# A decoder layer on one core: raw weight blocks of the summed operands on GpSimd's DMA queue, another split of the buffers, and sums three chunks ahead

## The chip, the cores and the metric

The kernel runs on one core of one Trainium2 chip. The time is the device time of one execution in microseconds (us); of several runs the median counts. The engines are called PE (TensorE, the matrix multiplications; PEld is its loading of weights), DVE (VectorE), ACT (ScalarE), POOL (GpSimd) and SP (SyncE, which here only issues DMAs). POOL issues DMAs too, through a queue of its own.

## The reference

One decoder layer for 256 tokens of width 2048, all in float32. `h = rmsnorm(x)` is multiplied by one wide matrix `w_in`, and the product is cut into seven parts:

```python
x_r, g_r, q, k, v, gate_r, gate_a = jnp.split(h @ w_in, ...)
y_r = (gelu(g_r) * rg_lru(conv(x_r), ...)) @ w_rnn_out
y_a = stick_breaking_attention(norm(q), norm(k), v) @ w_attn_out
x = x + (sigmoid(gate_r) * y_r + sigmoid(gate_a) * y_a) @ w_o
g, u = jnp.split(rmsnorm(x) @ w_ffn_gu, 2)
x = x + (silu(g) * u) @ w_ffn_down
x = x + sigmoid(rmsnorm(x) @ w_ple_gate) * (p @ w_ple_proj)
```

The weights are by far most of the bytes: about 400 MB cross from HBM in one execution.

## The kernel before

**Precision.** Each float32 weight `w` is cut on the chip into `whi = round(w)` (ACT, line 347) and `wlo = w - whi` (DVE, line 348), both in a shorter format that PE multiplies fast. Activations are cut in the same way. A product is then three matmuls: hi with hi, hi with lo, lo with hi (lines 622 to 624).

**Stages.** The order of the weights is fixed by `plan()`: first a gate (`gtr`), then the recurrent branch (loops over 11 pairs of column tiles), then the stages of `tail()`: `ro` (out of the recurrent branch), `v`, eight blocks for q and k with the attention between them, four blocks for the attention's gate (`gta`), `ao` (attention out), `wo`, and the FFN: groups `gu` 0 to 3, `dn0`, `gu` 4 to 7, `dn1`, `gu` 8 to 10, `dn2`; at last `pg`. A stage of the tail has one or two groups of columns, and a group is a list of slots (`SEVEN3`, `SEVEN4`, `LONG`, `TWELVE`). A slot is a plain chunk of 1024 weight columns (512 KB), or one with a name ("11", "T1", "22", ("S", 2, p), ...).

**Sums.** The named slots are a Strassen-like scheme: seven products of half-size blocks take the place of eight, and for that sums of raw weight blocks are needed. `Stream.dma_to` (line 243) loads a raw block of such a slot into a buffer of the large kind ("Q"), with SP's queue like all other weights (line 263). `Stream.summed` (line 268) adds blocks on DVE (line 273). Further terms are added by `joins` (line 306): a DMA from POOL's queue that adds onto what lies in the buffer (line 310).

**Look-ahead.** For each chunk that PE takes, `need` (line 360) issues loads up to 8 chunks ahead, splits up to 4 chunks ahead and sums up to `SUMS_AHEAD` = 2 chunks beyond those splits. `EARLY` moves the raw blocks of some groups four chunks forward in the order of the loads. Plain weights go through 4 buffers `w32` and 5 pairs `whi`/`wlo`.

**Buffers.** All other tiles come from two kinds: 29 of 1024 columns ("Q", 4 KB a partition) and 21 of 512 columns ("H"). The kind is picked by the tag of `tl` (line 413): "C" and "T" are H, all others Q. The eight tiles of the attention's gate are H.

**Order.** The engines' lists are made by a scheduler when the program is built; within a list an engine goes strictly in order. `issue_after` pins a piece behind another instruction of the same engine; `behind_splits` (line 850) pins it behind the latest split.

**V.** The tiles of `v` are scaled by the tokens' norms and split again (lines 940 to 946): one ACT and one DVE instruction for each of 8 tiles, written after each of the two groups.

Of the kernel before, what the change touches and what calls it, by code (L numbers as in the profile page):

```python
# [31 lines left out]
NG = 11  # L32
# [7 lines left out]
TWO = (0, 1)  # L40
FOUR = ("gu", "v")
LAST_GROUP = ("pg", 1)
SUMS_AHEAD = 2
TURNED_FROM = {"ao": 5, "wo": 5, "pg": 5}
EARLY = {(n, g): 4 for n in ("ro", "v", "wo", "pg") for g in range(2)}
NEG = -1e30


# [8 lines left out]
def is_sum(x):  # L57

    return isinstance(x, str) or isinstance(x, tuple) and x[0] == "S"
# [14 lines left out]
C_XR, C_GR, C_Q, C_K, C_V, C_GTR, C_GTA = 0, 22, 44, 60, 76, 92, 108  # L74
# [155 lines left out]
CHUNK_OF = {PLAN[c[0]][0][1:]: j for j, c in enumerate(CHUNKS) if PLAN[c[0]][0][0] == "tok"}  # L230


class Stream:


    def __init__(self, nc, w, p32, phl, quad, ahead_dma, ahead_split):
        self.nc, self.w, self.quad = nc, w, quad
        self.p32, self.phl = p32, phl
        self.ad, self.asp = ahead_dma, ahead_split
        self.n_dma = self.n_sum = self.n_split = self.pos = 0  # L240
        self.raw, self.sums, self.of, self.parts, self.after = {}, {}, {}, {}, {}

    def dma_to(self, n):
        n = DMA_UPTO[min(n, len(CHUNKS))]
        while self.n_dma < n:
            j = DMA_ORDER[self.n_dma]
            i, a, b = CHUNKS[j]
            c = P * (b - a)
            mode = PLAN[i][0][3] if PLAN[i][0][0] == "tok" else 0
            if is_sum(mode):  # L250
                if c:
                    t = self.quad()
                    self.raw[PLAN[i][0][1:]] = t
            else:
                if j in HALVES:
                    t = self.raw[j - 1][1][:, 512:]
                    self.raw[j] = t, None
                else:
                    t = self.p32.tile([P, 1024], F32, tag="w32", name=f"w32_{j}")
                    self.raw[j] = t, t  # L260
            if c:
                src = self.w[OFFS[j]:OFFS[j] + P * c].rearrange("(p c) -> p c", p=P)
                self.nc.sync.dma_start(t[:, :c], src)
            self.n_dma += 1
            if j in self.after:
                self.after.pop(j)()

    def summed(self, key):


        *at, mode = key
        r = self.raw
        add = lambda o, a, b: self.nc.vector.tensor_tensor(o, a, b, ALU.add)  # L273
        g = lambda m: (*at, m)
        if isinstance(mode, tuple):
            _, i, p = mode
            if i == 2:
                y = r[g(("Y", p))] = self.quad()
                a, b = r.pop(g(("S", 1, p))), r[key]
                add(y[:, :512], a[:, :512], b[:, 512:])  # L280
                add(y[:, 512:], y[:, :512], b[:, :512])
                self.joins(b, 512, g(("S", 2, p)), 0)
                return y, 1024
            if i == 3:
                return r.pop(g(("S", 2, p))), 1024
# [12 lines left out]
        if mode == "T3":  # L298
            return r.pop(g("12")), 1024
        if mode == "T4":  # L300
            return r.pop(g("R")), 1024
        t = r[g("R")]
        add(t, t, r[g("22")])
        return t, 1024

# [94 lines left out]
def tile_hybrid_block(ctx: ExitStack, tc: tile.TileContext, xT: bass.AP, x: bass.AP, pT: bass.AP,  # L400
                      prm: bass.AP, w: bass.AP, out: bass.AP):
    nc = tc.nc
# [4 lines left out]
    stat = ctx.enter_context(tc.tile_pool(name="stat", bufs=2))  # L407
    pps = ctx.enter_context(tc.tile_pool(name="pps", bufs=8, space=bass.MemoryType.PSUM))

    NT = {"Q": (29, 1024), "H": (21, 512)}  # L410
    cnt = [0]

    def tl(tag, dt=F32):
        cnt[0] += 1
        tag = "H" if tag in "CT" else "Q"
        n, c = NT[tag]
        return act.tile([P, c], dt, tag=tag, name=f"{tag}_{cnt[0]}", bufs=n)
# [5 lines left out]
    def f32(ap):  # L423
        return ap.bitcast(F32)
# [4 lines left out]
    def stt(o, a, s, b, op0, op1):  # L429
        nc.vector.scalar_tensor_tensor(o, a, s, b, op0, op1)  # L430

    def actv(o, i, f, **kw):
        nc.scalar.activation(o, i, f, **kw)  # L433

    S_ = Stream(nc, w, p32, phl, lambda: tl("X"), 4, 4)

    def load_x(t, i):
        nc.sync.dma_start(t, xT[:, 2 * i:2 * i + 2, :].rearrange("p k s -> p (k s)"))
# [27 lines left out]
    warm = psum()  # L466
    for i in range(8):
        nc.tensor.matmul(warm, blank[:, :P], blank, start=True, stop=True)
    ones = cst.tile([P, P], F32, tag="ones", name="ones")
    with tc.issue_after(m.ins):  # L470
        nc.vector.memset(ones, 1.0)
    eps_t = cst.tile([P, 1], F32, tag="eps", name="eps_t")
# [3 lines left out]
    zero_t = cst.tile([P, 1], F32, tag="zero", name="zero_t")  # L476
    nc.vector.memset(zero_t, 0.0)

    ones_r = cst.tile([P, P], F32R, tag="onesr", name="ones_r")
    nc.vector.tensor_copy(ones_r, ones)  # L480
    tmp = tl("T")
    later_r = cst.tile([P, P], F32R, tag="laterr", name="later_r")
    nc.gpsimd.affine_select(tmp[:, :P], ones, [[-1, P]], ALU.is_gt, 0.0, base=0, channel_multiplier=1)
# [180 lines left out]
    xg = []  # L664
# [172 lines left out]
    def rs_x(t):  # L837
        return rstd_tok[:, t:t + 1]

    def sigmoids(pss, tag):  # L840
        ts = [tl(tag) for _ in range(2)]
        for t, ps in enumerate(pss):
            actv(ts[t], ps, AF.Sigmoid, scale=rs_x(t))
        return ts

    def gate(c0, b, tag, step=None):
        return sigmoids(block(c0, b, step), tag)

    @contextmanager
    def behind_splits():  # L850
        with tc.issue_after(S_.hi_ins.ins), tc.issue_after(S_.lo_ins.ins):
# [54 lines left out]
    def whole(at, pairs, sums, also=()):  # L906

        (q2, q4, q3, q8), t = group(at, pairs, sums, None, also)
        c11, c21, c12, c22 = t["11"], t["T2"], t["T1"], t["T3"]
        tt(c11, q2, c11, ALU.add)  # L910
        tt(c21, q4, c22, ALU.add)
        tt(c12, q3, c12, ALU.add)
        tt(c22, q8, c22, ALU.subtract)
        return c11, c21, c12, c22
# [21 lines left out]
            tt(o, c, o, ALU.mult)  # L936
    mix_r = gtr

    vs = []
    for g in range(2):  # L940
        for i, c in enumerate(whole(("v", g), xg, xsum)):
            r = rs_x(i % 2)
            v = tl("B", F32R)
            actv(v[:, :512], c, AF.Identity, scale=r)
            stt(v[:, 512:], c, r, f32(v[:, :512]), ALU.mult, ALU.subtract)
            vs.append(v)


    qs, ks, zst, ost = {}, {}, {}, []
# [126 lines left out]
        slot[0] += 1  # L1076

    for b in range(4):
        head_norms(C_Q, b, step)
        head_norms(C_K, b, step)  # L1080
    gta = [gate(C_GTA, b, "T", step) for b in range(4)]
    assert not at

    mix, msum = [], {}
# [238 lines left out]
```

## Time and profile before

| what | us |
|---|---|
| runs | 1864.57, 1865.04, 1867.91 |
| median of the runs | 1865.04 |
| the profiled execution, as timed | 1866.62 |
| span of the profiled execution | 1864.7 |
| PE busy in it | 1851.0 |
| DVE busy | 1486.3 |
| ACT busy | 1244.0 |
| POOL busy | 117.1 |

The profile is of one execution. Its span runs from the first to the last instruction; the time around it is 1.92 us. PE's busy time counts a matmul from start to modelled end, and these overlap; so a late matmul costs the distance of the starts, which is a little more than the idle time that the profile names.

### The profile page before, as it was taken

Reading aid. Unit: us, or ns where it says so; the run is one execution under the profiler, and the core shown is the slowest. Engines: PE = TensorE matmul, PEld = TensorE weight load, DVE = VectorE, ACT = ScalarE, POOL = GpSimd, SP = SyncE. Lnnn points to the kernel's source line nnn. Section 1 sums busy time; section 2 is a strip of 40 time slices with the busy share of each in tenths; the row PEclk is TensorE's granted clock in tenths of the full one; section 3 lists DMA queues with packets and bytes.
Section 4 is the critical chain, followed back from the end, with each engine's and each line's share of the span. In section 5 each row is a group of like instructions: output and inputs, shape, how many; then the busy total and the mean of one; then the engine's idle time right before and its main releaser. Section 6 shows DMA issues by size and latency. Waiting matters only on the chain.

```text
span 1864.7 us, 24660 instructions
## 1 busy us (share of the span) xinstructions
PE 1851.0 (99%) x8882; PEld 1550.7 (83%) x8882; DVE 1486.3 (80%) x1874; ACT 1244.0 (67%) x1672; POOL 117.1 (6%) x142
## 2 busy tenths in 40 slices
PE   9999999999999999999999999999999999999998
PEld 7899889888878888888888878888788888888887
DVE  7688887677887576667798988897888988889986
ACT  6587888775565566667666776665656665666774
POOL 0000000000010000000000011100111001011000
PEclk9999999999999999999999999999999999999999
DMA  8546555677866544556777878787877669678674
GB/s 285 183 175 185 192 188 198 244 234 212 308 152 201 189 167 148 168 166 238 211 237 241 280 231 254 223 270 251 268 238 234 207 221 334 191 223 255 197 236 147
DMA packets 121370, 409.64 MB, mean 220 GB/s; under 512 B 13600, under 2 KB 14240, under 8 KB 121248
## 3 DMA queue, kind: packets, MB, share of 16 engines
q1 hardware_dynamic: 101808, 359.82, 53.6%
q0 software_dynamic: 19296, 48.24, 15.0%
q8 instruction: 69, 1.13, 0.2%
q14 instruction: 53, 0.43, 0.1%
q10 hardware_dynamic: 144, 0.01, 0.0%
HBM read 405.92 MB, written 2.10 MB: 219 GB/s over the span
## 4 chain that ended last, share of the span: by engine, by line
PE 90%; DMA 4%; DVE 4%; issue 1%; ACT 1%; SPq 0%; DVEq 0%; ACTq 0%
PE ps L623 24%; PE ps L624 24%; PE ps L622 24%; PE ps L552 9%; PE ps L556 5%; DMA Q<-in_w_dram 2%; DMA w<-in_w_dram 2%; DVE wlo L348 2%; PE ps L536 1%; PE ps L535 1%; PE ps L534 1%; DVE H L427 1%; ACT whi L347 0%; PE ps L1198 0%; PE ps L979 0%
## 5 line engine op out<-in xcount | busy, mean ns | idle before, releaser
L623 PE MATMUL ps<-wlo,Q 128*128 128x512 f32 x2184 | 852.1, 391 | 4.8 <-DVE wlo L348 4.7
L624 PE MATMUL ps<-whi,Q 128*128 128x512 f32 x2184 | 849.2, 389 | 0.0
L622 PE MATMUL ps<-whi,Q 128*128 128x512 f32 x2184 | 774.9, 392 | 0.7 <-ACT H L433 0.6
L348 DVE TENSOR_TENSOR wlo<-w,whi 128x1024 fp32r<-128x1024 f32 (+2 forms) x495 | 594.6, 1212 | 201.4 <-ACT whi L347 198.7
L347 ACT ACTIVATE whi<-w 128x1024 fp32r<-128x1024 f32 (+2 forms) x495 | 513.9, 1047 | 221.7 <-PE ps L624 133.7
L347 ACT ACTIVATE whi<-Q 128x1024 fp32r<-128x1024 f32 (+1 forms) x343 | 342.5, 1005 | 265.3 <-PE ps L624 217.5
L623 PEld LDWEIGHTS ps<-wlo,Q 128*128 128x128 f32 x2184 | 410.3, 188 | 91.8 <-DVE wlo L348 8.8
L622 PEld LDWEIGHTS ps<-whi,Q 128*128 128x128 f32 x2184 | 409.8, 188 | 91.5 <-ACT whi L347 3.9
L624 PEld LDWEIGHTS ps<-whi,Q 128*128 128x128 f32 x2184 | 410.1, 188 | 84.1
L348 DVE TENSOR_TENSOR wlo<-Q,whi 128x1024 fp32r<-128x1024 f32 (+1 forms) x343 | 393.5, 1158 | 67.1 <-ACT whi L347 66.3
L310 POOL DMA_DIRECT2D Q<-in_w_dram x134 | 114.7, 856 | 1698.2 <-DVE Q L273 625.8
L552 PE MATMUL ps<-Q,whi 128*128 128x512 f32 x704 | 170.7, 392 | 0.0
L552 PEld LDWEIGHTS ps<-Q,whi 128*128 128x128 f32 x704 | 128.7, 188 | 24.5
L273 DVE TENSOR_TENSOR Q<-Q,Q 128x512 f32<-128x512 f32 (+1 forms) x134 | 117.8, 888 | 36.5 <-DMA Q<-in_w_dram 35.6
L433 ACT ACTIVATE H<-ps 128x512 f32<-128x512 f32 (+1 forms) x163 | 84.5, 533 | 42.8 <-PE ps L624 31.5
L427 DVE TENSOR_TENSOR H<-H,H 128x512 f32<-128x512 f32 (+2 forms) x197 | 109.9, 570 | 1.2 <-ACT H L433 0.8
L427 DVE TENSOR_TENSOR H<-ps,H 128x512 f32<-128x512 f32 (+1 forms) x154 | 89.3, 606 | 20.5 <-PE ps L624 15.8
L556 PEld LDWEIGHTS ps<-Q,wlo 128*128 128x128 f32 x704 | 90.4, 191 | 3.5
L556 PE MATMUL ps<-Q,wlo 128*128 128x256 f32 x704 | 91.5, 283 | 0.0
L433 ACT ACT_TABLE_LOAD x53 | 68.0, 1283 | 1.8 <-DVE Q L427 0.7
L433 ACT ACTIVATE Q<-H 128x512 fp32r<-128x512 f32 x61 | 37.3, 625 | 33.2 <-DVE H L427 32.6
L427 DVE TENSOR_TENSOR Q<-H,Q 128x512 fp32r<-128x512 f32 x61 | 41.6, 689 | 0.7 <-ACT Q L433 0.7
(121 smaller groups left out, 900.3 us busy)
## 6 DMA issues: line engine op xcount, KB each, us to landing
w<-in_w_dram SPq DMA_DIRECT2D x471, 512.0 KB, 4.4
Q<-in_w_dram SPq DMA_DIRECT2D x184, 512.0 KB, 7.9
Q<-in_w_dram POOLq DMA_DIRECT2D x50, 512.0 KB, 7.4
Q<-in_w_dram POOLq DMA_DIRECT2D x84, 256.0 KB, 4.9
w<-in_w_dram SPq DMA_DIRECT2D x16, 448.0 KB, 3.2
H<-in_x_dram SPq DMA_DIRECT2D x8, 256.0 KB, 7.5
H<-in_xT_dram SPq DMA_DIRECT2D x7, 256.0 KB, 6.9
out_dram<-H SPq DMA_DIRECT2D x7, 256.0 KB, 4.4
```

What stands on the lines that cost most here:

```text
L273: add = lambda o, a, b: self.nc.vector.tensor_tensor(o, a, b, ALU.add)
L310: self.nc.gpsimd.dma_start(t[:, c:], src[:, a:a + 1024 - c], accum_op=ALU.add)
L347: self.hi_ins = self.nc.scalar.activation(h, t[:, :c], AF.Copy)
L348: self.lo_ins = self.nc.vector.tensor_tensor(l, t[:, :c], h.bitcast(F32), ALU.subtract)
L427: nc.vector.tensor_tensor(o, a, b, op)
L433: nc.scalar.activation(o, i, f, **kw)
L534: nc.tensor.matmul(o, wt[0], xh, start=start, stop=False)
L552: nc.tensor.matmul(pss[e], wt[0], rhs(xs, k), start=(k == 0), stop=(k == n - 1))
L556: nc.tensor.matmul(pss[e][:, :256], wt[1], rhs(xs, k)[:, :256], start=False, stop=False)
L622: nc.tensor.matmul(ps, x[0], wh, start=start, stop=False, skip_group_check=goes_on)
L623: nc.tensor.matmul(ps, x[0], wl, start=False, stop=False, skip_group_check=goes_on)
L624: nc.tensor.matmul(ps, x[1], wh, start=False, stop=stop, skip_group_check=goes_on)
```

## The change

1. Raw blocks of summed slots are issued by POOL's queue (`self.nc.gpsimd`), the plain weights stay on SP's. The loads of `x` that hang on certain weight loads (`self.after`) are pinned behind them on SP.
2. There are 31 large buffers and 18 small ones. The attention's gate is put into four large tiles, two blocks side by side.
3. `SUMS_AHEAD` is 3. `EARLY` also moves the raw blocks of the `gu` groups (all but 0, 4 and 8) three chunks forward. The sum for slot "T2" first has the loads issued up to its block "22".
4. `v` is scaled by `next_v`, called at slots 9, 11, 13 and 15 of the second `v` group for the first four tiles, and at steps 1, 3, 5, 7 of the first q block for the others.
5. The constant tile `ones` is a view of `ones_r` and is no longer copied.

```diff
-SUMS_AHEAD = 2
+SUMS_AHEAD = 3
-EARLY = {(n, g): 4 for n in ("ro", "v", "wo", "pg") for g in range(2)}
+EARLY = {**{(n, g): 4 for n in ("ro", "v", "wo", "pg") for g in range(2)},
+         **{("gu", g): 3 for g in range(NG) if g not in (0, 4, 8)}}
...
-                self.nc.sync.dma_start(t[:, :c], src)
+                q = self.nc.gpsimd if is_sum(mode) else self.nc.sync
+                d = q.dma_start(t[:, :c], src)
             self.n_dma += 1
             if j in self.after:
-                self.after.pop(j)()
+                with self.tc.issue_after(d.ins):
+                    self.after.pop(j)()
...
         t = r[g("R")]
+        self.dma_to(CHUNK_OF[g("22")] + 1)
         add(t, t, r[g("22")])
...
-    NT = {"Q": (29, 1024), "H": (21, 512)}
+    NT = {"Q": (31, 1024), "H": (18, 512)}
...
-    ones = cst.tile([P, P], F32, tag="ones", name="ones")
+    ones_r = cst.tile([P, P], F32R, tag="onesr", name="ones_r")
+    ones = f32(ones_r)
...
+    def next_v():
+        c, r = vc.pop(0), rs_x(len(vs) % 2)
+        v = tl("B", F32R)
+        actv(v[:, :512], c, AF.Identity, scale=r)
+        stt(v[:, 512:], c, r, f32(v[:, :512]), ALU.mult, ALU.subtract)
+        vs.append(v)
+
     for g in range(2):
-        for i, c in enumerate(whole(("v", g), xg, xsum)):
...
+        vc.extend(whole(("v", g), xg, xsum, {9 + 2 * i: next_v for i in range(4)} if g else {}))
...
     for b in range(4):
+        if b == 0:
+            for i in range(4):
+                at.setdefault(1 + 2 * i, []).append((lambda _: next_v(), 0))
...
-    gta = [gate(C_GTA, b, "T", step) for b in range(4)]
+    for b in range(4):
+        pss = block(C_GTA, b, step)
+        if b % 2 == 0:
+            wide_ = [tl("X") for _ in range(2)]
+        gta.append([t[:, b % 2 * 512:b % 2 * 512 + 512] for t in wide_])
+        for t, ps in enumerate(pss):
+            actv(gta[b][t], ps, AF.Sigmoid, scale=rs_x(t))
```

More of the change, by code (lines that the diff above doesn't have):

```diff
@@ L233, with __init__ @@
 class Stream:
-    def __init__(self, nc, w, p32, phl, quad, ahead_dma, ahead_split):
-        self.nc, self.w, self.quad = nc, w, quad
+    def __init__(self, tc, w, p32, phl, quad, ahead_dma, ahead_split):
+        self.tc, self.nc, self.w, self.quad = tc, tc.nc, w, quad
         self.p32, self.phl = p32, phl
@@ L433, in actv @@
         nc.scalar.activation(o, i, f, **kw)
-    S_ = Stream(nc, w, p32, phl, lambda: tl("X"), 4, 4)
+    S_ = Stream(tc, w, p32, phl, lambda: tl("X"), 4, 4)
     def load_x(t, i):
@@ L477, in tile_hybrid_block @@
     nc.vector.memset(zero_t, 0.0)
-    ones_r = cst.tile([P, P], F32R, tag="onesr", name="ones_r")
-    nc.vector.tensor_copy(ones_r, ones)
     tmp = tl("T")
@@ L844, in sigmoids @@
         return ts
-    def gate(c0, b, tag, step=None):
-        return sigmoids(block(c0, b, step), tag)
     @contextmanager
@@ L937, in tile_hybrid_block @@
     mix_r = gtr
-    vs = []
-    for g in range(2):
-        for i, c in enumerate(whole(("v", g), xg, xsum)):
[L942 to L946, printed above, removed]
+    vs, vc = [], []
+    def next_v():
[4 more added lines that the diff above has]
+        vs.append(v)
+    for g in range(2):
+        vc.extend(whole(("v", g), xg, xsum, {9 + 2 * i: next_v for i in range(4)} if g else {}))
     qs, ks, zst, ost = {}, {}, {}, []
@@ L1078, in tile_hybrid_block @@
     for b in range(4):
+        if b == 0:
+            for i in range(4):
+                at.setdefault(1 + 2 * i, []).append((lambda _: next_v(), 0))
         head_norms(C_Q, b, step)
         head_norms(C_K, b, step)
[L1081 removed]
+    gta = []
+    for b in range(4):
[5 more added lines that the diff above has]
+            actv(gta[b][t], ps, AF.Sigmoid, scale=rs_x(t))
     assert not at
```

## The prediction

> **What bounds the kernel now.** I read the page's busy times and its chain first, then a table of stages (columns: window, length, and busy time with count for PE, PEld, DVE, ACT, POOL, then granted clock, DMA share, GB/s), then PE's timeline at the places where PE stands still.
>
> ```profile
> span 1864.7 us, 24660 instructions
> PE 1851.0 (99%) x8882; PEld 1550.7 (83%) x8882; DVE 1486.3 (80%) x1874; ACT 1244.0 (67%) x1672; POOL 117.1 (6%) x142
> q1 hardware_dynamic: 101808, 359.82, 53.6%
> q0 software_dynamic: 19296, 48.24, 15.0%
> PE 90%; DMA 4%; DVE 4%; issue 1%; ACT 1%; SPq 0%; DVEq 0%; ACTq 0%
> ```
> ```profile
> 555.00:1000.00 445.00, 445.00 (x2120) 373.00 (x2119) 322.97 (x410) 289.76 (x458) 13.41 (x16) 1.00 0.60 193
> 1240.00:1330.00 90.00, 88.21 (x386) 71.98 (x386) 72.95 (x78) 51.33 (x56) 10.25 (x12) 1.00 0.87 281
> 1540.00:1580.00 40.00, 39.33 (x174) 32.25 (x173) 32.28 (x36) 22.85 (x24) 4.98 (x6) 1.00 1.01 354
> 1820.00:1864.70 44.70, 38.20 (x180) 31.92 (x179) 28.36 (x35) 19.58 (x25) 0.65 (x1) 0.96 0.43 140
> ```
>
> PE is the bound: 1851.0 of 1864.7 us busy, at full clock, and the diff leaves its 8882 matmuls as they are. So the change can win only where PE stands idle, 13.7 us in all. Of these 6.5 us are the last stage (44.70 - 38.20), after the last load, which the diff doesn't touch. In the long q/k stage from 555 to 1000 PE has no idle time at all, with DMA at 60%. Idle time gathers where DMA is nearly full: 1.79 us at 1240 to 1330 (87%), 0.67 us at 1540 to 1580 (101%).
>
> What one wait costs is read from PE's timeline (start, length, idle before it in brackets with its releaser), beside one row of the chain with PE at its pace.
>
> ```profile
> 72.92 3.65 PE ps L552 x16
> 514.03 0.50 PE L623 MATMUL ps<-wlo,Q 128*128 128x512 f32 x1 [0.29 <-DVE wlo L348]
> 514.37 0.40 PE L624 MATMUL ps<-whi,Q 128*128 128x512 f32 x1
> 516.37 0.50 PE L623 MATMUL ps<-wlo,Q 128*128 128x512 f32 x1 [0.69 <-DVE wlo L348]
> 1079.37 0.50 PE L622 MATMUL ps<-whi,Q 128*128 128x512 f32 x1 [0.56 <-ACT H L433]
> 1278.53 0.50 PE L623 MATMUL ps<-wlo,Q 128*128 128x512 f32 x1 [0.25 <-DVE wlo L348]
> 1281.46 0.50 PE L623 MATMUL ps<-wlo,Q 128*128 128x512 f32 x1 [0.37 <-DVE wlo L348]
> 1323.96 0.50 PE L623 MATMUL ps<-wlo,Q 128*128 128x512 f32 x1 [1.18 <-DVE wlo L348]
> 1428.27 0.39 PE L622 MATMUL ps<-whi,Q 128*128 128x512 f32 x1
> 1428.76 0.50 PE L623 MATMUL ps<-wlo,Q 128*128 128x512 f32 x1
> 1577.72 0.50 PE L623 MATMUL ps<-wlo,Q 128*128 128x512 f32 x1 [0.67 <-DVE wlo L348]
> ```
>
> Matmuls start every 3.65/16 = 0.228 us and are shown 0.39 us long, so the bracket misses 0.39 - 0.23 = 0.16 us of each wait; the matmul behind a wait comes 514.37 - 514.03 = 0.34 us later, another 0.11. A wait costs its bracket + 0.27 us. So the places are worth: A (v) 0.29 + 0.69 + 0.54 = 1.5; B (gu 0) 0.56 + 0.27 = 0.8; C (dn0) 0.25 + 0.37 + 0.54 = 1.2; D (dn0's second group) 1.18 + 0.27 = 1.45; E (gu 6, 1428.76 - 1428.27 - 0.23 + 0.11) 0.4; F (dn1's second group) 0.67 + 0.27 = 0.9. Together **6.3 us**, the most that earlier raw blocks can give.
>
> What makes D late, from the chain, DVE's timeline and the waits (total us, times, longest):
>
> ```profile
> 1309.36 12.63 DMA Q<-in_w_dram
> 1322.08 0.69 DVE L273 TENSOR_TENSOR Q<-Q,Q 128x512 f32<-128x512 f32 x1 [2.66 <-DMA Q<-in_w_dram]
> 1322.69 2.35 DVE L348 TENSOR_TENSOR wlo<-Q,whi 128x1024 fp32r<-128x1024 f32 x2
> DVE Q L273 <- DMA Q<-in_w_dram: 35.6, 16, 4.6
> ```
>
> A raw block is issued at 1309.36 and lands 12.63 us later, at 1321.99. DVE, idle for 2.66 us, starts the sum at 1322.08; the split follows, and PE gets its `wlo` at 1323.96. This is the pattern: SP's one queue issues raw blocks late, for each waits until a large buffer is free, and then many cross together. DVE waited 35.6 us in 16 such places, most of it without harm to PE.
>
> **The change part by part.**
>
> ```profile
> L310 POOL DMA_DIRECT2D Q<-in_w_dram x134 | 114.7, 856 | 1698.2 <-DVE Q L273 625.8
> Q<-in_w_dram SPq DMA_DIRECT2D x184, 512.0 KB, 7.9
> ```
>
> *Raw blocks on POOL's queue.* 184 loads of 512 KB leave SP for POOL. POOL gets 184 × 0.856 = 158 us of issuing more: 117 → 275 us, 15% of the span. POOL is on no path now, so the issuing itself costs 0. SP's plain weights no longer stand behind a raw that waits for a buffer, and a raw that waits holds only POOL's list; that is what moves A to F. The other side: raws now share a list with 134 joins, each of which waits for a sum on DVE.
>
> A cover to doubt is DVE beside a busy POOL. Rows of one lo-split with and without a POOL issue beside it:
>
> ```profile
> 483.28 1.23 DVE L348 TENSOR_TENSOR wlo<-w,whi 128x1024 fp32r<-128x1024 f32 x1
> 489.38 0.85 POOL L310 DMA_DIRECT2D Q<-in_w_dram  x1 [31.22 <-ACT whi L347]
> 489.50 1.23 DVE L348 TENSOR_TENSOR wlo<-w,whi 128x1024 fp32r<-128x1024 f32 x1
> ```
>
> Both take 1.23 us: 0 for DVE. The Trainium skill, "GPSIMD Engine Reference", section "Key points", has the two engines share their way into SBUF and contend when a DVE instruction reads two operands there; by that the 158 us of issuing could stretch such splits, but the row beside an issue isn't longer, and I charge nothing.
>
> *What a plain copy of POOL's queue costs the DMA engines* is in no row; both bounds come from the two queues. q1 took 53.6% for 359.82 MB, 0.149% per MB; q0, with joins only, 15.0% for 48.24 MB, 0.311% per MB, 2.09 times as much. A join also reads and adds, a plain raw doesn't, so the nearest row is SP's identical copy: I take 1.0 times, cost 0; at 2.09 the 184 × 0.524 = 96.5 MB add 96.5 × 0.162 = 15.6% of DMA time (rival C).
>
> *Sums three ahead, EARLY for seven gu groups, raw "22" before the T2 sum.* In the built lists raws stand earlier in most groups and sums a chunk earlier. One chunk more at 12 or more matmuls is 12 × 0.228 = 2.7 us of lead or more. That exceeds each wait of A, B, C, E (0.69 us at most), where I take back all or nearly all: A 1.5, B 0.6 (its releaser is an ACT evacuation, so only what lies behind a late split goes), C 1.2, E 0.4. Bounds: 0 and the full 3.9.
>
> *D and F* need care, since lists decide. In the second group of dn0 and of dn1, POOL's list reads join, raw, join, then seven raws; so eight raws stand behind joins. DVE's list has the T2 sums (2 × 0.69) ahead of three evacuations, one wide sum and two splits before the split that PE awaits.
>
> ```profile
> 1314.67 0.69 DVE L427 TENSOR_TENSOR H<-ps,H 128x512 f32<-128x512 f32 x1
> 1301.83 0.86 POOL L310 DMA_DIRECT2D Q<-in_w_dram  x1 [16.32 <-DVE Q L273]
> 1305.26 0.85 POOL L310 DMA_DIRECT2D Q<-in_w_dram  x1 [2.57 <-DVE Q L273]
> ```
>
> That work is 1.4 + 3 × 0.69 + some 1.3 (a wide sum, as a split of that width) + 2.35 = 7.1 us. PE wants the split's result at 1323.96 - 1.45 = 1322.5, so the raw must land by about 1322.5 - 7.1 = 1315.4; each us later is 1 us of PE. The joins were issued at 1301.83 and 1305.26, the first after 16.32 us of waiting for DVE. If they keep these times, eight raws, the joins (one raw's worth) and about four plain loads cross behind the first: 13 × 0.524 MB at 354 GB/s (1.48 us each) = 19 us, landing at 1301 + 19 = 1320, 4.5 us late. Sums a chunk earlier bring the joins 3 to 7 us forward: 1313 to 1317. I take the middle, 1315, with some loss left: D 0.8 back of 1.45, F 0.5 of 0.9. Bounds for each: all back, and 4.5 us lost.
>
> *31 large and 18 small buffers, the gate in large tiles.* PE's busy time in the stage 555 to 1000 shows no wait for any tile; the four large gate tiles leave 27 instead of 29 for the rest while the gate lives, while raws are issued farther ahead. Cost 0; bounds: -0.5 us (an earlier raw) and +1 (a raw held as long as one of A's waits).
>
> *V scaled behind splits.*
>
> ```profile
> L430 DVE SCALAR_TENSOR_TENSOR Q<-H,rstd_tok,Q 128x512 fp32r<-128x512 f32 x8 | 5.7, 748 | 0.0
> L433 ACT ACTIVATE Q<-H,rstd_tok 128x512 fp32r<-128x512 f32 x8 | 5.5, 714 | 0.6 <-DVE H L427 0.6
> ```
>
> 5.7 us of DVE and 5.5 us of ACT don't go, they move out of the v groups' ends into gaps; part of A's recovery is theirs. Cover: splits up to four chunks ahead. Without it up to 0.75 us once.
>
> *The start of wo.* In the built lists the transposes of its operand stand nearer to their first use, about 2.0 us instead of 3.7.
>
> ```profile
> L433 ACT ACTIVATE H<-ps 128x512 f32<-128x512 f32 (+1 forms) x163 | 84.5, 533 | 42.8 <-PE ps L624 31.5
> L433 ACT ACTIVATE Q<-H 128x512 fp32r<-128x512 f32 x61 | 37.3, 625 | 33.2 <-DVE H L427 32.6
> ```
>
> In between must lie a copy (0.53), a rounding (0.62) and a lo part on DVE (0.69): 1.84 plus hand-overs, close to 2.0. I take +0.4, bounds 0 and 1.0.
>
> *The start.*
>
> ```profile
> 5.50 0.22 DVE L480 CAST ones_r<-ones 128x128 fp32r<-128x128 f32 x1
> 4.09 6.65 DMA w<-in_w_dram
> ```
>
> The 0.22 us cast goes; it lies under a weight load from 4.09 to 10.74. That load stands ahead of the pinned x loads too: 0, bounds -0.2 and +1.
>
> **Sum.** -1.5 - 0.6 - 1.2 - 0.8 - 0.4 - 0.5 + 0.4 = -4.6 us. The profiled execution's 1866.62 (span 1864.7) becomes 1862.0. It lies 1.58 above the median 1865.04, so the median becomes **1860.4**.
>
> **Rivals.**
>
> *A: the transfers were hidden or full anyway.* At C, D and F DMA is at 87 to 101%; a second queue adds no bandwidth, so raws issued earlier land no earlier. Then A, C, D and F stay, mostly; B and E go and a part of A: -0.6 - 0.4 - 1.4 + 0.4 = -2.0, **1863.0**. For it: the 101% and 354 GB/s. Against: before both stages DMA is at 60 to 80%, so the burst can spread forward, if buffers allow. The Trainium skill, "DMA: Bandwidth & Descriptors", section "Issuing engines are not separate DMA queues", says that DMAs of all issuing engines run on the same engines and only issue time is saved; that is this rival, and the full stages agree with it.
>
> *B: slower, the head of POOL's list.* Place: the second groups of dn0 and dn1, where eight raws wait behind two joins. Price: 4.5 us each instead of 1.45 and 0.9, +3.1 + 3.6. A and C stay, B and E go: +6.7 - 1.0 + 0.4 = +6.1, **1871.1**. It decides as soon as the raws land after 1315.4 + 1.4, when the stall passes that of before; it ends over 1868.8 when they land after about 1319. For it: the 16.32 us that the first join waited for DVE. Against: the sums are a chunk earlier.
>
> *C: plain raws on POOL's queue cost as much as joins.* The stretch from 1000 to 1820 in the table of stages, and its raw loads:
>
> ```profile
> 1000.00:1820.00 820.00, 816.22 (x3646) 668.76 (x3645) 703.63 (x819) 532.71 (x655) 86.60 (x102) 1.00 0.78 242
> Q<-in_w_dram SPq DMA_DIRECT2D x132, 512.0 KB, 8.0
> ```
>
> 132 × 0.524 MB × 0.162% × 1864.7 us = 209 us of DMA time on top of 0.78 × 820 = 640: 849 us in a stretch of 820, 29 us more, **1894**. Against: a join has an addition, a raw has none.
>
> That the change does nothing at all is counted with A.
>
> **How the numbers follow.** About 0.2% (3.7 us) is what a measurement of this kernel can tell from no change: faster ends at 1861.3, slower begins at 1868.8. Forecast 0.46, nearly all below 1861.3 (say 0.45, the rest to same); A 0.29, same; B 0.19, slower for the most part; C 0.06, slower. Faster 0.45, same 0.31, slower 0.24. Range: lowest is all of 6.3 back and the 1.58 us of spread between the profiled run and the median as margin, 1857.0; upward through A and most of B, to 1870.0. Outside stay C, the upper part of B, and a little below: 2 in 10. The forecast's own range is 1858 to 1862.
>
> **What would show it.** POOL near 275 us with 318 issues of raws and joins; PE's waits at 514, 1079, 1278 and 1428 gone or under 0.1 us; D and F under 0.7 us; the wait of DVE's sums for raws well under 35.6 us in total. For A: the same waits, with raws issued earlier and under way longer than 7.9 us. For B: PE waiting several us near 1323 and 1577 and POOL waiting for DVE just ahead. For C: q0 above 40% of DMA time. The forecast is wrong if a wait of over 2 us appears at any place where there was none.

## The result and the profile after

The changed kernel takes 1868.51 us (median of 18 runs, 1866.8 to 1872.62), the kernel before 1864.74 us in 18 runs beside it (1863.27 to 1867.91). The ratio is 1.002, 95% interval 1.0013 to 1.0027: **3.8 us slower**, where 4.6 us faster was forecast. The profiled execution of the changed kernel took 1868.08 us.

Its page: busy times, queues, chain, the joins (L314), the raw loads on POOL (L265), DVE's sums (L276) and the loads' landing.

```profile
span 1866.3 us, 24635 instructions
PE 1851.1 (99%) x8882; PEld 1551.2 (83%) x8882; DVE 1488.2 (80%) x1873; ACT 1242.1 (67%) x1672; POOL 219.9 (12%) x326
q1 hardware_dynamic: 75312, 263.34, 39.9%
q0 software_dynamic: 45792, 144.72, 28.7%
PE 92%; DVE 2%; DMA 2%; ACT 1%; issue 1%; SPq 0%; POOL 0%; ACTq 0%; DVEq 0%; POOLq 0%
L314 POOL DMA_DIRECT2D Q<-in_w_dram x134 | 119.0, 900 | 951.8 <-DVE Q L276 708.9
L265 POOL DMA_DIRECT2D Q<-in_w_dram x184 | 113.8, 754 | 645.5 <-PE ps L1041 274.9
L276 DVE TENSOR_TENSOR Q<-Q,Q 128x512 f32<-128x512 f32 (+1 forms) x134 | 118.0, 886 | 25.7 <-DMA Q<-in_w_dram 24.8
Q<-in_w_dram POOLq DMA_DIRECT2D x234, 512.0 KB, 8.4
```

DMA is a smaller part of the chain (2% after 4%), and DVE's sums wait 24.8 us for raw blocks instead of 35.6. That alone doesn't show that the raws come earlier, as was meant: a sum that stands later in DVE's list also waits less, and the experiments show such a shift. Meanwhile PE waits at other places and for other engines. Rows of PE's timeline with a wait, at the places that the prediction names and at the starts of gu 0, dn0 and dn1:

```profile
516.36 0.50 PE L626 MATMUL ps<-wlo,Q 128*128 128x512 f32 x1 [0.20 <-DVE wlo L352]
1071.64 0.50 PE L625 MATMUL ps<-whi,Q 128*128 128x512 f32 x1 [0.70 <-ACT whi L351]
1076.48 0.97 PE L625 MATMUL ps<-whi,Q 128*128 128x512 f32 x3 [0.70 <-ACT whi L351]
1239.05 0.73 PE L625 MATMUL ps<-whi,Q 128*128 128x512 f32 x2 [1.30 <-ACT whi L351]
1324.34 0.50 PE L626 MATMUL ps<-wlo,Q 128*128 128x512 f32 x1 [0.38 <-DVE wlo L352]
1493.35 0.73 PE L625 MATMUL ps<-whi,Q 128*128 128x512 f32 x2 [1.30 <-ACT whi L351]
1579.20 0.50 PE L626 MATMUL ps<-wlo,Q 128*128 128x512 f32 x1 [0.95 <-DVE wlo L352]
```

The waits at 1278 and 1428 are gone, and of the two at 514 and 516 one is left, and smaller. New are two waits for ACT's `whi` at the start of gu 0 and one of 1.30 us at the start of dn0 (1239) and of dn1 (1493).

All these kernels have the same 8882 matmuls, so the start of the n-th matmul can be compared with that of the n-th in the first profile of before. Where nothing differs the distance stays the same to 0.02 us for hundreds of microseconds, so what a place wins (-) or loses (+) reads off cleanly. The times in the first column are those of the first profile of before; experiments are described below. Places that differ by less are left out; they come to some 0.1 us in all, in e1 to 0.4. Each column is one execution: those of e1, e9, e14 and e16 took 2.7, 1.6, 0.9 and 0.4 us less than the medians of their kernels, those of e10 and e15 3.1 and 2.2 us more, so the distance of two columns can overstate what a kernel gains or loses.

| place, us | before again (e11) | changed | changed again (e12) | e1 | e9 | e15 | e10 | e16 |
|---|---|---|---|---|---|---|---|---|
| start, 2 to 16 | -0.86 | -0.63 | +0.43 | -0.84 | -0.85 | +0.22 | -0.77 | -0.59 |
| A: v, 505 to 525 | -0.31 | -0.91 | -0.91 | -1.35 | -1.40 | -0.51 | -0.91 | -1.14 |
| gu 0 (with B), 1050 to 1085 | -0.01 | +1.25 | +1.25 | +1.23 | +1.23 | +1.27 | +1.23 | +1.27 |
| gu 1 to 3, 1115 to 1205 | -0.04 | +1.13 | +0.09 | 0.00 | -0.03 | +0.16 | +2.47 | -0.01 |
| dn0's start, 1232 to 1242 | -0.01 | +0.95 | +0.95 | +0.95 | -0.01 | 0.00 | -0.01 | -0.01 |
| C: dn0, 1270 to 1290 | -1.21 | -1.21 | -1.21 | -1.21 | -1.21 | -1.21 | -1.21 | -1.21 |
| D: dn0's second group, 1316 to 1335 | -1.02 | -0.41 | +0.38 | -1.51 | -1.51 | +0.08 | +0.17 | -1.51 |
| gu 4 to 6 (with E), 1335 to 1440 | +0.64 | -0.51 | -0.45 | -0.50 | -0.47 | -0.49 | -0.49 | -0.50 |
| dn1's start, 1485 to 1500 | +0.01 | +0.95 | +2.53 | +0.95 | -0.01 | +0.03 | -0.01 | -0.01 |
| F: dn1's second group, 1560 to 1590 | +0.38 | +0.63 | +0.21 | -0.99 | -0.92 | +0.41 | +1.04 | -0.99 |
| gu 8 and 9, 1590 to 1660 | +0.81 | +0.23 | +0.46 | +0.04 | +0.15 | +2.08 | +0.89 | +0.32 |
| span | -1.62 | +1.64 | +3.89 | -2.82 | -4.99 | +2.16 | +2.57 | -4.27 |

The column "before again" is the first lesson: a second execution of the *unchanged* kernel lacks the waits at C and E altogether (at E it wins 0.40 us, and loses 1.04 elsewhere between 1335 and 1420), and has a smaller one at D. Its PE waits at A, D and F:

```profile
515.21 0.50 PE L623 MATMUL ps<-wlo,Q 128*128 128x512 f32 x1 [0.68 <-DVE wlo L348]
1320.53 0.50 PE L623 MATMUL ps<-wlo,Q 128*128 128x512 f32 x1 [0.18 <-DVE wlo L348]
1575.28 0.50 PE L623 MATMUL ps<-wlo,Q 128*128 128x512 f32 x1 [1.04 <-DVE wlo L348]
```

So 1.6 of the forecast's 4.6 us (C and E) were an accident of the one execution that it read. The wait at C stands in none of the other traces.

### The profile page after: what moved, and what is told of

Same layout as the page of the kernel before. It is cut to its first block, busy times and chain, and to the rows that moved or that the text cites. A ratio compares the mean times of both kernels' runs of the same rounds, so it can differ in the third digit from the quotient of the medians.

```text
span 1866.3 us, 24635 instructions
## 1 busy us (share of the span) xinstructions
PE 1851.1 (99%) x8882; PEld 1551.2 (83%) x8882; DVE 1488.2 (80%) x1873; ACT 1242.1 (67%) x1672; POOL 219.9 (12%) x326
## 3 DMA queue, kind: packets, MB, share of 16 engines
q1 hardware_dynamic: 75312, 263.34, 39.9%
q8 instruction: 69, 1.13, 0.2%
## 4 chain that ended last, share of the span: by engine, by line
PE 92%; DVE 2%; DMA 2%; ACT 1%; issue 1%; SPq 0%; POOL 0%; ACTq 0%; DVEq 0%; POOLq 0%
PE ps L626 25%; PE ps L627 25%; PE ps L625 25%; PE ps L555 9%; PE ps L559 5%; DMA Q<-in_w_dram 2%; PE ps L539 1%; PE ps L538 1%; PE ps L537 1%; DVE wlo L352 1%; ACT whi L351 1%; DVE H L431 1%; DVE Q L276 1%; PE ps L1211 0%; PE ps L982 0%
## 5 line engine op out<-in xcount | busy, mean ns | idle before, releaser
L314 POOL DMA_DIRECT2D Q<-in_w_dram x134 | 119.0, 900 | 951.8 <-DVE Q L276 708.9
L265 POOL DMA_DIRECT2D Q<-in_w_dram x184 | 113.8, 754 | 645.5 <-PE ps L1041 274.9
L276 DVE TENSOR_TENSOR Q<-Q,Q 128x512 f32<-128x512 f32 (+1 forms) x134 | 118.0, 886 | 25.7 <-DMA Q<-in_w_dram 24.8
L431 DVE TENSOR_TENSOR H<-H,H 128x512 f32<-128x512 f32 (+2 forms) x181 | 98.9, 556 | 0.8 <-ACT H L437 0.5
```

The source lines that it names most:

```text
L265: d = q.dma_start(t[:, :c], src)
L314: self.nc.gpsimd.dma_start(t[:, c:], src[:, a:a + 1024 - c], accum_op=ALU.add)
L431: nc.vector.tensor_tensor(o, a, b, op)
```

## The experiments

Ratios are to the kernel before, run beside each; +-0.0009 is the half width of an interval, so a difference of two ratios is known to about 2.4 us, and the places in the table tell more than the times do.

| run | ratio (95% interval) | median us, before beside it |
|---|---|---|
| e1 queue only | 0.9997 (0.9988 to 1.0005) | 1866.34, 1866.19 |
| e2 raws on SP | 0.9995 (0.9986 to 1.0004) | 1865.52, 1866.19 |
| e3 dn raws on SP | 0.9999 (0.999 to 1.0008) | 1866.92, 1866.19 |
| e4 dn, gu 0, wo raws on SP | 1.0001 (0.9992 to 1.001) | 1866.05, 1866.19 |
| e5 changed, two ahead | 1.0015 (1.0006 to 1.0024) | 1868.08, 1865.35 |
| e6 queue for some | 0.998 (0.9971 to 0.9989) | 1861.47, 1865.35 |
| e7 e4 with two ahead | 1.0004 (0.9995 to 1.0012) | 1865.64, 1865.35 |
| e8 changed, no EARLY for gu | 1.0016 (1.0007 to 1.0025) | 1868.24, 1865.35 |
| e9 queue only, pinned | 0.9987 (0.9978 to 0.9996) | 1863.0, 1865.63 |
| e10 changed, pinned | 1.0002 (0.9993 to 1.0011) | 1865.93, 1865.63 |
| e13 e10 with two ahead | 0.9993 (0.9984 to 1.0002) | 1865.78, 1865.83 |
| e14 e9 with three ahead | 0.9984 (0.9975 to 0.9993) | 1862.91, 1865.83 |
| e15 e9 with the new buffers | 1.0003 (0.9994 to 1.0012) | 1866.41, 1866.07 |
| e16 e10 with the old buffers | 0.9982 (0.9973 to 0.999) | 1862.54, 1866.07 |

### Which part of the change: the queue or the rest (e1, e2)

e1 is the kernel before with the raws on POOL's queue:

```diff
-                self.nc.sync.dma_start(t[:, :c], src)
+                q = self.nc.gpsimd if is_sum(mode) else self.nc.sync
+                q.dma_start(t[:, :c], src)
```

> The kernel before with one edit: raw blocks go through POOL's queue. Its built lists show the same reordering as the changed kernel at the start of gu 0 (ACT takes the norm's table loads ahead of two splits) and at the starts of dn0 and dn1 (DVE adds dn's first sum some 3 us later, PE takes all eight transposes first). Theory L (the lists): in the changed kernel these three places cost 1.2 + 1.5 + 1.5 = 4.2 us more of PE's time than before, and they come with the queue alone. Without sums three ahead little of A to F is won back, so 2 to 5 us slower than before, with PE waiting over 1 us for whi near 1072, 1238 and 1493. Rival H (raws standing behind joins in POOL's list): also slower, but the new waits are at gu 3, dn0's and dn1's second groups, and the three places cost nothing. Rival S (buffers, EARLY or sums three ahead do the harm): within 1 us of before.

Equal to before, so theory L failed on the sum. The table does show its three places, with the same loss as in the changed kernel to 0.02 us: +1.23, +0.95 and +0.95 (1.2, 1.5 and 1.5 were expected). What it had missed is that the queue wins A, D and F back in full.

How it wins D and F is in DVE's list, not in earlier raws. In the kernel before, the sum that waits for its raw at D (1322.08, shown in the prediction) stands ahead of the two splits that PE needs. In e1 it stands behind them, and while it still waits for DMA, PE doesn't:

```profile
1318.79 2.35 DVE L349 TENSOR_TENSOR wlo<-Q,whi 128x1024 fp32r<-128x1024 f32 x2
1321.70 0.69 DVE L274 TENSOR_TENSOR Q<-Q,Q 128x512 f32<-128x512 f32 x1 [0.56 <-DMA Q<-in_w_dram]
```

F is alike: before, the sum (1575.83, after 2.15 us of waiting) is ahead of the splits; in e1 the splits (1571.72) are ahead of the sum (1573.99). The kernel e9, described below, shows that the raws themselves are no earlier: its sums at D and F start at 1320.33 and 1572.30, both after a wait for DMA (0.90 and 0.35 us), while PE is there 2.26 and 4.16 us ahead of before. Counted from PE's work in the first profile of before, that is 1322.6 and 1576.5, against 1322.08 and 1575.83. This is read from the traces; no run pins these splits. At A, too, the half sum that waits before (509.81) has moved behind a split; whether its raw lands earlier isn't shown.

e2 is the changed kernel with `q = self.nc.sync` for all blocks.

> The changed kernel with one part undone: raw blocks are issued by SP's queue again. All else stays (31 and 18 buffers, EARLY, sums three ahead, V behind splits). Its lists at gu 0, dn0 and dn1 are those of before. Theory L: the 4.2 us of the three places go, most of what A, C, D and E won by earlier sums stays: 1 to 4 us faster than before, 5 us or more faster than the changed kernel. Rival H: like L in time, but PE's waits at gu 3, at 1327 and at 1579 go and those at 1238 and 1493 stay. Rival S: 3 to 5 us slower than before, like the changed kernel.

4.7 us faster than the changed kernel by the ratios (0.0025 of 1865), and equal to before within the interval, so theory L's 1 to 4 us under before isn't shown. Gu 0 and the dn starts lose nothing (+0.01, -0.01, -0.02), but v loses 2.51 us: a sum that waits 3.09 us for its raw (at 508.42) stands there ahead of evacuations and splits. Queue alone and the rest alone each leave the time as it was; together they cost 0.2%.

### The order of the lists (e3, e4, e6, e9, e10)

Why would a queue cost time at the start of dn0, where nothing waits for DMA? The changed kernel there, DVE's, ACT's and PE's timelines:

```profile
1234.18 0.68 DVE L276 TENSOR_TENSOR Q<-Q,Q 128x512 f32<-128x512 f32 x1
1234.78 0.74 DVE L434 SCALAR_TENSOR_TENSOR H<-H,rs,H 128x512 f32<-128x512 f32 x1
...
1236.05 0.74 DVE L434 SCALAR_TENSOR_TENSOR H<-H,rs,H 128x512 f32<-128x512 f32 x1
1236.71 1.82 DVE L276 TENSOR_TENSOR Q<-Q,Q 128x512 f32<-128x512 f32 x2
```
```profile
1237.45 0.60 ACT L437 ACTIVATE Q<-ps 128x512 fp32r<-128x512 f32 x1 [3.29 <-PE ps L1211]
1237.95 1.05 ACT L351 ACTIVATE whi<-Q 128x1024 fp32r<-128x1024 f32 x1
```
```profile
1236.71 1.03 PE L1211 MATMUL ps<-ident,H 128*128 128x128 f32 x8
1239.05 0.73 PE L625 MATMUL ps<-whi,Q 128*128 128x512 f32 x2 [1.30 <-ACT whi L351]
```

And before:

```profile
1233.81 0.68 DVE L273 TENSOR_TENSOR Q<-Q,Q 128x512 f32<-128x512 f32 x1
1234.41 0.75 DVE L430 SCALAR_TENSOR_TENSOR H<-H,rs,H 128x512 f32<-128x512 f32 x1
```
```profile
1234.59 1.06 ACT L347 ACTIVATE whi<-Q 128x1024 fp32r<-128x1024 f32 x1 [1.45 <-DVE Q L273]
```

Before, the second half of the half sum starts at 1233.81, ahead of the products with the token scales (L430), and ACT splits it at 1234.59. After the change it starts at 1236.71, behind those products (L434); ACT idles 3.29 us for PE's transposes and splits at 1237.95; PE, whose list now has all eight transposes together, waits 1.30 us. DVE has no DMA wait in this stretch: the operands were there. Only the order in the built lists differs. The scheduler makes that order, and as e1 shows, the queue of the raws alone changes it. At gu 0 ACT's list changes likewise: the table load of the norm goes ahead of splits. No run pins this place, so its cause is read from the lists and from e1 and e2, which differ there as their lists do. After, then before:

```profile
1068.32 1.28 ACT L437 ACT_TABLE_LOAD   x1
...
1070.53 2.00 ACT L351 ACTIVATE whi<-Q 128x1024 fp32r<-128x1024 f32 x2
```
```profile
1068.20 1.06 ACT L347 ACTIVATE whi<-Q 128x1024 fp32r<-128x1024 f32 x1
...
1073.10 1.28 ACT L433 ACT_TABLE_LOAD   x1
```

e3 and e4 put some raws of the changed kernel back on SP, e6 does as e4 with the kernel before (the edit, shortened):

```diff
-                q = self.nc.gpsimd if is_sum(mode) else self.nc.sync
+                # e3: only dn0 and dn1; e4, e6: with wo and gu 0
+                q = self.nc.gpsimd if is_sum(mode) and not (PLAN[i][0][1] == "wo" or PLAN[i][0][1:3] in {
+                    ("gu", 0), ("dn0", 0), ("dn1", 0)}) else self.nc.sync
```

> The changed kernel, where only the raw blocks of the first groups of dn0 and dn1 (12 loads) go back to SP's queue; 172 stay on POOL's. In the built lists the order at the starts of dn0 and dn1 is that of before, that of gu 0 stays as changed. Theory L: PE's waits at 1238 and 1493 go, 2 x 1.5 = 3 us faster than the changed kernel, so within 1.5 us of before. Rival H: the raws behind joins elsewhere stay, under 1 us of difference from the changed kernel.

As L has it: 0.9999, which is 3.9 us faster than the changed kernel, and 0.00 and -0.02 us at the dn starts, with 12 loads moved.

> The changed kernel, where the raw blocks of wo, of gu 0 and of the first groups of dn0 and dn1 (32 loads) go back to SP's queue. The order of the lists at gu 0, dn0 and dn1 is then that of before at all three places. Theory L: 4 us faster than the changed kernel, so 0 to 2 us faster than before; what is left of loss is at gu 3 and in dn1's second group. Rival H: under 1.5 us of difference from the changed kernel.

3.5 us faster than the changed kernel, though not faster than before: gu 0 still loses 0.54 us and dn1's second group 2.11.

> The kernel before, raw blocks on POOL's queue except those of wo, gu 0 and the first groups of dn0 and dn1 (these 32 stay on SP's); nothing else changed. In the built lists gu 0, dn0 and dn1 start as before. Theory L (lists): against queue alone the 1.25 + 0.95 + 0.95 us go and the gains at v, dn0, gu 6 and dn1 stay: 2 to 4 us faster than before. Rival H (raws behind joins): the raws left on POOL's queue wait as in queue alone, so within 1 us of it and of before.

0.998, 3.7 us faster than before: L again. Gu 0 loses 0.91 us although ACT's list there is that of before. The trace has the raw for that: PE comes to gu 0 about 2 us earlier than before, the raw on SP's queue only 0.8 us earlier (DVE's wide sum starts at 1065.63 after 2.66 us of waiting, before at 1066.45 after 1.34), and PE then waits 0.59 us for DVE at 1073.64.

e9 tests the order with queue and transfers left alone. It takes e1 and pins, behind gu 3 and gu 7, the two products behind the second half of the half sum (recorded as `adds` in `summed`, traced ahead by one `sum_to`; `half` stands for the key of its slot):

```diff
+        if g in (3, 7):
+            S_.sum_to(CHUNK_OF[half] + 1)
...
-            stt(c, c, rs1[:, t:t + 1], s_, ALU.mult, ALU.mult)
+            with tc.issue_after(S_.adds[half].ins) if g in (3, 7) else nullcontext():
+                stt(c, c, rs1[:, t:t + 1], s_, ALU.mult, ALU.mult)
```

> Queue alone (all 184 raw blocks on POOL's queue, the rest as before) with one pin: after gu 3 and gu 7, DVE's two products with the token scales stand behind the two halves of the first half sum of the next dn group, as their list had them in the kernel before. Queue and transfers are those of queue alone. Theory L (the order of the lists, not the queue, costs the time at the dn starts): PE's added 0.95 us in each of 1232 to 1242 and 1485 to 1500 falls under 0.3 us; gu 0's 1.2 us stays; 1.3 to 1.9 us faster than queue alone. Rival H (the raw lands later by POOL's queue): both stay at 0.95 us or more, DVE then waits for DMA at the sum.

The dn starts: +0.95 to -0.01, both. Time 0.9987 against e1's 0.9997 (1.9 us, which by the times alone wouldn't be clear of noise). DVE, then PE, of e9 at dn0's start:

```profile
1233.37 0.69 DVE L275 TENSOR_TENSOR Q<-Q,Q 128x512 f32<-128x512 f32 x1
1233.97 1.41 DVE L432 SCALAR_TENSOR_TENSOR H<-H,rs,H 128x512 f32<-128x512 f32 x2
```
```profile
1237.70 0.50 PE L625 MATMUL ps<-wlo,Q 128*128 128x512 f32 x1 [0.35 <-DVE wlo L350]
```

The sum stands ahead of the products again, and PE's wait is as small as before. That the order, not the queue, costs the time at the dn starts is shown.

> The changed kernel with the same pin at the starts of dn0 and dn1, nothing else. Theory L: the added 0.95 us at each start goes, 1.3 to 1.9 us faster than the changed kernel, 1 to 3 us slower than before, with the waits at gu 0, gu 3 and in dn1's second group unchanged. Rival H: no change from the changed kernel.

1.0002: 3.4 us faster than the changed kernel, more than the 1.9 us of the two starts, and not the expected 1 to 3 us slower than before. A part of the rest is a dip of PE's clock (last section).

### The second groups of dn0 and dn1 (e5, e7, e8, e13 to e16)

With the starts repaired, e10 still lies 0.0015 above e9. The table shows where: D, F and gu 1 to 3. My first theory was that sums three ahead do it.

```diff
-SUMS_AHEAD = 3
+SUMS_AHEAD = 2
```

> The changed kernel with SUMS_AHEAD at 2 again; the queue, buffers, EARLY and V stay as changed. Theory P (sums three ahead put a DVE sum that waits for a raw ahead of splits that PE needs sooner): PE's extra waits at gu 3 (1160 to 1205, 1.1 us), and what is lost against queue alone in the second groups of dn0 (1.1 us) and dn1 (1.6 us) go; the three places with reordered lists (gu 0, starts of dn0 and dn1, 1.25 + 0.95 + 0.95 us) stay: some 3.5 us faster than the changed kernel, equal to before within 1 us. Rival E (EARLY or the buffers delay those raws): no more than 1 us from the changed kernel, 3 to 4 us slower than before.

Against the expectation no gain (1.0015). Gu 1 to 3 and F came back (+0.12, -0.78), but each dn start lost 2.5 us, with a dip of PE's clock at each (last section). e7 makes the same edit in e4:

> The changed kernel with both remedies: sums two chunks ahead, and the raw blocks of wo, gu 0 and the first groups of dn0 and dn1 on SP's queue; 31 and 18 buffers, EARLY and V behind splits stay. Theories L and P together: PE's added waits at gu 0, gu 3, both dn starts and in the second groups go, 3.2 + 3.5 = 6.7 us faster than the changed kernel, 3 us faster than before. If only one of the two holds, half of it: equal to before within 1 us.

1.0004, equal to before, as expected if only one of the two theories holds; D didn't come back (-0.01).

> The changed kernel without EARLY for the gu groups (their raw blocks stand again in the order of use); sums three ahead, queue, buffers and V stay. Theory P: the waits at gu 3 and in the second groups of dn0 and dn1 stay or grow, within 1 us of the changed kernel or up to 2 us slower. Rival E: these waits go, 2 to 3.5 us faster than the changed kernel.

1.0016: not EARLY (e8 drops its gu entries). To get the starts out of the way, e13 is e10 with two ahead, and e14 is e9 with three ahead and the early load of block 22:

> The changed kernel with the pin at the dn starts and SUMS_AHEAD 2; queue, buffers, EARLY and V as changed. Theory P + L: nothing at the dn starts and no dip of the clock there, no waits at gu 3, and the second groups of dn0 and dn1 lose at least 1 us less than in the changed kernel with the pin alone: 2 to 4 us faster than that one, 1 to 3 us faster than before. Rival E (buffers, EARLY or V cost what is left): no faster than the changed kernel with the pin alone, equal to before within 1 us.

0.9993, 1.7 us faster than e10, which isn't clear of noise. F is 1.0 us better than in e10 (+0.04), but D isn't (+0.45): half of what P needs.

> Queue alone with the pin, and sums three ahead (with the early load of block 22); buffers, EARLY and V as before. Theory P: PE's waits come back in the second groups of dn0 (1.1 us or more) and dn1 (1.2 us or more) against queue alone pinned, gu 3 in some executions: 2 to 4 us slower than it, equal to before within 1.5 us. Rival E: within 1 us of queue alone pinned, 2.5 us faster than before.

0.9984, D -1.51, F -0.77: three ahead alone costs nothing. **Theory P fell** as the cause by itself. Whether three ahead adds to a loss at F once the buffers are changed stays open: with the new buffers and all or most raws on POOL's queue, F is at -0.78, -0.74, +0.04 and +0.41 with two ahead (e5, e7, e13, e15), and at -0.01 to +2.11 with three (e8, e12, changed, e3, e10, e4). What is left is the buffers. e15 adds them to e9 (with the gate in large tiles and the `ones` view, since otherwise they don't fit), e16 takes buffers and gate tiles out of e10:

```diff
-    NT = {"Q": (29, 1024), "H": (21, 512)}
+    NT = {"Q": (31, 1024), "H": (18, 512)}
...
+            wide_ = [tl("X") for _ in range(2)]
```

> Queue alone with the pin, plus 31 large and 18 small buffers, the attention's gate in four large tiles, and no copied ones tile (without it the buffers don't fit). Sums two ahead, EARLY and V as before. Theory B (the buffers): PE's waits come back in the second groups of dn0 (1.1 us or more) and dn1 (0.9 us or more) and some at v: 2 to 4 us slower than queue alone pinned, equal to before within 1.5 us. Rival E (EARLY or V): within 1 us of queue alone pinned, 2 us or more faster than before.

> The changed kernel with the pin and with the buffers of before (29 large, 21 small, the attention's gate in small ones); the queue, sums three ahead, EARLY, V and the ones view stay. Theory B: the waits at gu 3 and in the second groups of dn0 and dn1 go: 2 to 4 us faster than the changed kernel with the pin, 2 to 3 us faster than before, like queue alone pinned. Rival E: no faster than the changed kernel with the pin, within 1 us of before.

1.0003 against 0.9987 and 0.9982 against 1.0002: the buffers cost 3.0 us in one kernel and 3.7 in the other, each known to about 2.4 us. Their number and the gate's tiles were changed together, so which of the two does it isn't separated. Sums three ahead, EARLY for gu and V are all in e16, so none of them costs; against e9 (0.9987) they also win nothing that is clear of noise. DVE at D, with the new buffers (e15), and PE's wait behind it:

```profile
1317.07 0.69 DVE L275 TENSOR_TENSOR Q<-Q,Q 128x512 f32<-128x512 f32 x1 [1.65 <-DMA Q<-in_w_dram]
...
1321.81 1.21 DVE L275 TENSOR_TENSOR Q<-Q,Q 128x1024 f32<-128x1024 f32 x1
1322.95 2.35 DVE L350 TENSOR_TENSOR wlo<-Q,whi 128x1024 fp32r<-128x1024 f32 x2
```
```profile
1324.21 0.50 PE L624 MATMUL ps<-wlo,Q 128*128 128x512 f32 x1 [0.92 <-DVE wlo L350]
```

and with the old (e16), where PE doesn't wait:

```profile
1317.77 2.35 DVE L353 TENSOR_TENSOR wlo<-Q,whi 128x1024 fp32r<-128x1024 f32 x2
1320.71 0.69 DVE L277 TENSOR_TENSOR Q<-Q,Q 128x512 f32<-128x512 f32 x1 [0.59 <-DMA Q<-in_w_dram]
```

With the new buffers the half sum stands *ahead* of the two splits that PE needs at 1323, and DVE idles 1.65 us there for a raw; with the old ones (and the raws on POOL's queue) the splits go first and the wait for the raw falls behind them. At F the lists differ in the same way (in e15 the half sum waits 1.46 us at 1570.75, ahead of the splits at 1576.63). The order of the lists again, this time set by the buffers.

### Two more profiles (e11, e12)

> The kernel before once more, for a second profile of it. If the places A, D and F are the same in each execution, PE loses 1.6, 1.45 and 0.95 us there again; if they hang on how the transfers fall in one execution, they differ by 0.5 us or more, and the profile that the prediction used was a poor draw of them, since its 1866.62 us lay above the median.

> The changed kernel once more, for a second profile of it. The added 1.25 us at gu 0 and 0.95 us at each dn start are the same to 0.1 us if lists cause them. The waits at gu 3 and in the second groups of dn0 and dn1 (1.1, 1.0 and 1.6 us), which follow transfers, may differ by 0.5 us or more.

Of the three places that the first expectation names, only D differs by more than 0.5 us (1.02; A by 0.31, F by 0.38). C and E, which it doesn't name, differ by 1.2 and 0.4. In the changed kernel, gu 1 to 3 differ by 1.0, D by 0.8 and F by 0.4. So what follows transfers is in part chance. What follows the lists repeats: gu 0 +1.25 twice, dn0's start +0.95 twice. Dn1's start misses the expected 0.1 us with +2.53 in e12, for the reason in the last section.

## Why the prediction was wrong, point by point

Two steps of the sum failed, and a third, the mechanism of the gain, was wrong though its size was nearly right.

- **The step on the buffers**: "Cost 0; bounds: -0.5 us ... and +1". They cost 3.0 and 3.7 us. The prediction looked for tiles that PE waits for and found none; what the buffers change is the order that the scheduler gives DVE's list.
- **The sum's list of moved instructions**: it counted one place where the built lists differ (wo, +0.4; measured +0.01 from 960 to 1050) and left out three others, gu 0, where 0.6 back was forecast and 1.25 was lost, and the starts of dn0 and dn1, 0.95 each. Together that is 3.75 us of the 6.2 us between the forecast of -4.6 and the +1.64 of the first profile after.
- **The mechanism of the gain**: plain weights no longer behind a raw that waits, and so earlier raws, were to move A to F. The queue alone does win A (-1.40 in e9), D (-1.51) and F (-0.92), but at D and F the raws land no earlier; the waiting sum stands behind the splits in DVE's list. That the sizes come near 1.5, 1.45 and 0.9 is luck.
- **D and F**: 0.8 and 0.5 back were forecast; measured -0.41 and +0.38 at D, +0.63 and +0.21 at F. Here the prediction had read the order in DVE's list rightly, without seeing that it came with the buffers, and its rule holds: PE is 0.7 us later there than before, so the raw was due by 1316.1; the sum starts at 1317.19 and in e12 at 1318.04, 1.1 and 1.9 us late, and PE loses 1.04 and 1.83 us there (1.45 less 0.41, and 1.45 plus 0.38). What was mis-sized is the landing, taken as 1315. The joins did go out early (1294.73 and 1296.54, 7 us earlier than before), but the raw was issued only at 1305.44, after waits for PE's work, and took 11.72 us.
- **C and E** (1.2 and 0.4 back) were in no way the change's: e11 lacks them too. "The most that earlier raw blocks can give" was the most in one execution. The last step, 1.58 us from the profiled execution to the median, in part took the wait at C off a second time.
- **A**: 0.9 back for 1.5; with the queue alone it is 1.40, and the new buffers take a part (e15: 0.51).
- **Rival A** has its premise borne out at D and F, where the raws land no earlier in e9. Its conclusion fails: D and F win all the same, through the order of DVE's list.
- **Rival B** had the place and the sign, and its time (1871.1) is the nearest to the measured one. That is partly luck, since it has neither gu 0 nor the dn starts, which lose 3.15 us. Its mechanism, raws held behind two joins, isn't what the traces show: POOL waits 4.00 and 0.37 us ahead of the joins, and the raw comes 9 us after them. Its price of 4.5 us a place is too high: column e10 less e16 gives 1.7 us at D and 2.0 at F, and e10's column is an execution 3.1 us above its median.
- **Rival C** is excluded: q0 rose by 96.48 MB and 13.7% of DMA time, 0.142% per MB, as q1 (39.9% for 263.34 MB, 0.152%). The Trainium skill, "DMA: Bandwidth & Descriptors", section "Issuing engines are not separate DMA queues", has all issuers share the same DMA engines; the equal price per MB agrees. What the change gains beyond issue time comes from another order of DVE's list.
- POOL is busy 219.9 us, not 275: the raws' 184 issues keep it busy for 113.8 us, 0.62 us each, against 0.89 for a join in the same profile (119.0 us for 134). The rows' means of one issue (754 and 900 ns) are longer, since some overlap.

## What to carry to other kernels

Where a scheduler orders the engines' lists, a change of queue or of buffer counts is also a change of those lists: compare the built lists at every place where they differ, ACT and PE too, and price each as a wait of the bound engine. Here a sum that had to wait for its data did no harm behind the splits that PE needed next, and cost time ahead of them. When PE is at 99%, take a second profile of the unchanged kernel before counting its waits as gain. The version to keep has the queue, the old buffers, and the lists of before at the dn starts: e6 (0.998), e16 (0.9982), e14 (0.9984) and e9 (0.9987) all beat both kernels and can't be told apart.

## What the runs showed of the hardware that was not expected

A wait of 1.30 us can bring PE's clock down. In e12, at dn1's start, the table of windows (PE, PEld, DVE, ACT, POOL busy, then granted clock, DMA share, GB/s) and a matmul in it:

```profile
1490.00:1495.00 5.00, 3.62 (x19) 2.55 (x18) 5.00 (x8) 2.40 (x4) 2.49 (x4) 1.00 0.60 125
1495.00:1500.00 5.00, 4.86 (x14) 3.85 (x15) 5.00 (x6) 4.85 (x7) 1.76 (x2) 0.66 0.94 280
1500.00:1505.00 5.00, 5.00 (x23) 4.14 (x23) 3.52 (x5) 2.71 (x4) 0.87 (x2) 1.00 1.05 281
```
```profile
1496.68 0.63 PE L626 MATMUL ps<-wlo,Q 128*128 128x512 f32 x1
```

The granted clock is 0.66 over 5 us, and matmuls start every 0.43 us (1496.68 to 1497.10) instead of 0.228: 1.58 us more, which makes 2.53 of 0.95. A narrower window, 1496.08 to 1499.49, has the clock at 0.50: it is half speed for 3.41 us. In the 3.41 us ahead of it, PE is busy for 1.89. e5 has the dip at both dn starts (0.66 at 1240 to 1245 and at 1495 to 1500). In the five profiles with the reordered starts (changed, e12, e1, e5, e8) it follows 3 of 10 starts; in the other profiles, with the old order or the pin, none. How long PE is busy doesn't decide it alone: at dn0's start of the same e12, PE is busy for 1.89 of 3.41 us as well (1236.65 to 1240.06), and the clock stays at 1.00. The Trainium skill, "TensorE: Matmul & The Clock Gate", section "What's actually happening", has the clock halve after an idle window of about 3.4 us that runs freely. That it comes at some starts only agrees with a free-running window; that 1.30 us of idle time, behind eight small transposes, is enough doesn't follow from the page.

The mean clock of every execution shows how often this comes. A dip of 3.41 us at half speed takes about 0.001 off the mean, and 8 of 18 executions of the changed kernel have 0.998 or less, with a median of 1869.07 us against 1867.76 of the other ten. None of e10's 11 executions has it, nor any of the 128 of the kernel before. So the dips are a part of the 3.4 us between e10 and the changed kernel; how much of it isn't known more closely.
